# The FFN's second projection as seven half-block products, its steps placed between the next chunk's up-projection items

## Chip, cores and metric

The kernel runs on one core of one Trainium2 chip, in one launch. The metric is the device time of one execution in microseconds; lower is better. Before the change it is 1301.34 us, the median of three runs (1300.74 to 1302.6).

## The reference

The model is a decoder trunk with two layers, on 512 tokens of width 1024, all in fp32. Each layer has a token mixer (gated linear attention in the first, gated DeltaNet in the second) and then a feed-forward network, the FFN. This change touches the FFN and the residual ahead of it:

```python
def conv_ffn(x, w_in, conv_w, w_out):
    h = causal_dwconv(x @ w_in, conv_w)          # width 3, per channel
    gate, up = jnp.split(h, 2, axis=-1)
    return (jax.nn.gelu(gate, approximate=False) * up) @ w_out

h = layer_norm(ALPHA * h + y, ln_g[i, 0], ln_b[i, 0])                  # y: the mixer's output
h = layer_norm(ALPHA * h + conv_ffn(h, ...), ln_g[i, 1], ln_b[i, 1])
```

`w_in` is 1024 x 5632 and `w_out` 2816 x 1024. The hidden width 2816 is 22 blocks of 128.

## The kernel before

An fp32 product is made of three matmuls. Each operand is split into a high part, cast to fp32r on ACT (ScalarE), and a low part, the difference, taken on DVE (VectorE); PE (TensorE) adds high x high, high x low and low x high in one PSUM bank. So every weight costs one cast (L243, or L233 for pieces of 512 columns) and one subtraction (L244, L234), and so does every activation that is multiplied (`split_out`, L416 to L418).

The FFN (`ffn`, L646) works in two chunks of 12 and 10 blocks. For a block f there are two *items*, gate and up: 24 matmuls of 512 columns each (`fm_mms`, L286; the tiles are called `fm`), which leave one block of 128 channels by 512 tokens in one PSUM bank. `ffn_conv` (L637) applies the three taps of the convolution, one on ACT (L641) and two on DVE (L643). The gate goes through gelu on ACT (L653). The up item is multiplied by it on DVE (L658) and split into `gh` and `gl`.

When a chunk's items are done, `out_proj` (L370) multiplies its blocks by the rows of `w_out` that belong to them, for each half of the 1024 output columns and each of four blocks of 128 tokens (`tm_half`, L342; tiles `tm`). It adds the result to the residual `h` from PSUM (L379 the first time, L381 later). In the last chunk the last half ends token block by token block (`tail`, with `TAIL` = 4 weight pairs held in small slots, L229). Behind each token block come its statistics (L386) and the layer norm: `ln` (L542) transposes the result for the next stage, `ln_out` (L588) writes the output.

The weights follow one list, `plan`, in the order of use. `weight()` takes the next entry, and `prefetch` (L262) issues the load on SP's queue and the split for as many entries ahead as `look` says (2, or 8 near the end of an FFN), as long as fewer than `WB` = 4 weight buffers are held. Small work, such as a layer norm's, is a generator with due times that `pump` (L126) advances between matmuls by a planner's clock. After the first stage `pin` is off (L813). From there the order of an engine's instructions is that of the program only as far as the framework that compiles it keeps to it.

`ln` also prepares the residual for the FFN behind a mixer: scale and shift by the layer norm's parameters, two operations on POOL (GpSimd) for each half of a token block (L583, L584).

SBUF tiles of 128 x 512 fp32 come from one pool of 53 slots, and PSUM has eight banks.

## Time and profile before

| | |
|---|---|
| median of three runs | 1301.34 us |
| profiled execution, span on the core | 1300.2 us |
| PE busy, matmuls | 1279.0 us, 6666 |
| DVE, ACT, POOL busy | 790.2, 546.8, 111.0 us |
| first FFN on PE | from 241.1 to about 598 us |
| second FFN on PE | from 934.6 to about 1290 us |
| HBM read | 119.63 MB |

The profile is of one execution. Its page gives each engine's busy time, the chain of work that ended last (followed back from the last instruction), the costliest groups of instructions by line, engine and tile, and the DMA issues. The trace behind it can be asked for the chain in order of time, for the waits, for busy times by stretch and for single instructions. A row of a group reads: line, engine, operation, output<-input, shape and count | busy us in all, mean ns of one | idle time of the engine just before them, and what ended it. In a list of single instructions, the brackets at the end hold that idle time.

### The profile page before, as it was taken

What the parts mean: (1) busy time and instruction counts of PE and PEld (TensorE: products, weight loads), DVE (VectorE), ACT (ScalarE), POOL (GpSimd) and SP (SyncE); (2) the same over time, 40 slices, a digit from 0 to 9 for tenths busy, and PEclk for the clock granted to TensorE, in tenths of its full rate; (3) what the DMA queues carried; (4) which work ended last, traced back from release to release, by engine and by line L of the source; (5) the groups of instructions that cost most, each with busy time, mean ns of one, the idle gap of its engine ahead of it and who ended that gap; (6) DMA issues with size and microseconds to landing.
All of it is one profiled execution on the core that took longest, in us unless ns stands there. A gap on an engine that the chain in (4) does not pass through costs nothing.

```text
span 1300.2 us, 17238 instructions
## 1 busy us (share of the span) xinstructions
PE 1279.0 (98%) x6666; PEld 1078.1 (83%) x6666; DVE 790.2 (61%) x1442; ACT 546.8 (42%) x1030; POOL 111.0 (9%) x150
## 2 busy tenths in 40 slices
PE   8999999999999999999999999999999999999996
PEld 6878888988888888889788889988888888888885
DVE  3673366676643466655799835669677653366656
ACT  3554443634421344425865535543554431244420
POOL 4000000070000000001111310100034000000000
PEclk9999999999999999999999968999999999999999
DMA  6421224143333333251543420333143333333331
GB/s 181 117 81 49 77 86 130 33 130 114 98 97 97 97 97 98 87 143 66 135 117 106 127 49 17 115 98 113 49 137 107 97 98 98 97 97 97 97 98 65
DMA packets 167089, 126.52 MB, mean 97 GB/s; under 512 B 16088, under 2 KB 139546, under 8 KB 167008
## 3 DMA queue, kind: packets, MB, share of 16 engines
q1 hardware_dynamic: 161728, 115.10, 30.0%
q0 software_dynamic: 3888, 8.50, 2.1%
q10 hardware_dynamic: 1392, 1.84, 0.4%
q8 instruction: 52, 0.85, 0.3%
q14 instruction: 29, 0.24, 0.1%
HBM read 119.63 MB, written 5.78 MB: 96 GB/s over the span
## 4 chain that ended last, share of the span: by engine, by line
PE 86%; issue 6%; DVE 5%; DMA 1%; ACT 1%; POOL 1%; DVEq 0%; POOLq 0%; ACTq 0%
PE fm L155 45%; PE tm L155 32%; PE o L155 1%; PE V L155 1%; PE R L155 1%; PE xT L166 1%; PE vn L155 1%; DVE ln_st L386 1%; PE pg L155 1%; PE yT L166 1%; PE qkT L166 1%; PE pq L155 0%; DMA gla_nw<-in_gla_norm_w_dram 0%; DVE wl L244 0%; DVE conv L940 0%
## 5 line engine op out<-in xcount | busy, mean ns | idle before, releaser
L244 DVE TENSOR_TENSOR wl<-raw,wh 128x1024 fp32r<-128x1024 f32 (+1 forms) x190 | 238.3, 1255 | 321.1 <-ACT wh L243 319.3
L155 PE MATMUL fm<-xh,wh 128*128 128x512 f32 (+1 forms) x1104 | 408.3, 370 | 0.4 <-ACT wh L243 0.4
L155 PE MATMUL fm<-xl,wh 128*128 128x512 f32 (+1 forms) x1104 | 404.8, 367 | 0.0
L155 PE MATMUL fm<-xh,wl 128*128 128x512 f32 (+1 forms) x1096 | 401.2, 367 | 2.5 <-DVE wl L244 2.5
L243 ACT CAST wh<-raw 128x1024 fp32r<-128x1024 f32 (+1 forms) x190 | 198.8, 1047 | 269.9 <-PE tm L155 159.4
L155 PEld LDWEIGHTS fm<-xh,wl 128*128 128x128 f32 x1096 | 207.4, 190 | 36.5 <-DVE wl L244 3.1
L155 PEld LDWEIGHTS fm<-xh,wh 128*128 128x128 f32 x1104 | 209.1, 189 | 34.2 <-ACT wh L243 1.2
L155 PEld LDWEIGHTS fm<-xl,wh 128*128 128x128 f32 x1104 | 209.3, 190 | 32.7
L643 DVE SCALAR_TENSOR_TENSOR conv<-fm,ffn_cw,conv 128x511 f32<-128x511 f32 (+1 forms) x176 | 130.7, 745 | 3.0
L155 PE MATMUL tm<-wl,gh 128*128 128x512 f32 x288 | 112.0, 389 | 0.0
L155 PE MATMUL tm<-wh,gh 128*128 128x512 f32 x288 | 112.0, 389 | 0.0
L155 PE MATMUL tm<-wh,gl 128*128 128x512 f32 x288 | 112.0, 389 | 0.0
L155 PE MATMUL tm<-wh,xh 128*128 128x512 f32 x192 | 79.5, 414 | 1.0 <-ACT qk L756 1.0
L417 ACT CAST gh<-conv 128x512 fp32r<-128x512 f32 x44 | 27.3, 621 | 124.7 <-DVE conv L658 124.6
L155 PE MATMUL tm<-wh,xl 128*128 128x512 f32 x192 | 75.4, 393 | 0.0
L155 PE MATMUL tm<-wl,xh 128*128 128x512 f32 x192 | 75.1, 391 | 0.0
L653 ACT ACTIVATE conv<-conv 128x512 f32<-128x512 f32 x44 | 27.8, 633 | 95.0 <-DVE conv L643 95.0
L155 PEld LDWEIGHTS tm<-wh,gh 128*128 128x128 f32 x288 | 54.1, 188 | 11.2
L155 PEld LDWEIGHTS tm<-wh,gl 128*128 128x128 f32 x288 | 54.1, 188 | 11.2
L155 PEld LDWEIGHTS tm<-wl,gh 128*128 128x128 f32 x288 | 54.1, 188 | 11.2
L641 ACT ACTIVATE conv<-fm,ffn_cw 128x512 f32<-128x512 f32 x88 | 59.9, 681 | 0.2
L940 DVE SCALAR_TENSOR_TENSOR conv<-fm,gdn_cw,conv 128x509 f32<-128x509 f32 (+2 forms) x72 | 53.2, 742 | 4.6 <-ACT conv L938 4.1
(274 smaller groups left out, 1555.4 us busy)
## 6 DMA issues: line engine op xcount, KB each, us to landing
raw<-in_ffn_w_in_dram SPq DMA_DIRECT2D x88, 512.0 KB, 3.7
raw<-in_ffn_w_out_dram SPq DMA_DIRECT2D x44, 512.0 KB, 3.7
raw<-in_gdn_w_in_dram SPq DMA_DIRECT2D x32, 512.0 KB, 4.0
raw<-in_gla_w_in_dram SPq DMA_DIRECT2D x23, 512.0 KB, 3.5
raw<-in_gla_w_out_dram SPq DMA_DIRECT2D x8, 512.0 KB, 3.5
raw<-in_gdn_w_out_dram SPq DMA_DIRECT2D x8, 512.0 KB, 3.8
hd<-h POOLq DMA_DIRECT2D x8, 256.0 KB, 2.5
dt<-drow POOLq DMA_DIRECT2D x8, 256.0 KB, 5.6
```

The lines of the kernel that those rows point to most:

```text
L155: t = self.nc.tensor.matmul(out, a, b, start=start, stop=stop)
L166: t = self.nc.tensor.transpose(out, a, self.ident[:n, :n])
L243: nc.scalar.copy(wh[:, cols], raw[:, cols])
L244: nc.vector.tensor_sub(wl[:, cols], raw[:, cols], wh[:, cols])
L386: nc.vector.bn_stats(self.st[tb][:, hf, :], h)
L417: cast = self.nc.scalar.copy(dst_h, src)
L641: nc.scalar.activation(a, ps, AF.Identity, scale=tap(2))
L643: nc.vector.scalar_tensor_tensor(a[:, d:], ps[:, :S - d], tap(2 - d), a[:, d:], ALU.mult, ALU.add)
L653: nc.scalar.activation(a, a, AF.Gelu)
L940: self.conv = nc.vector.scalar_tensor_tensor(a[:, d:], ps[:, :S - d], tap(3 - d), a[:, d:], ALU.mult, ALU.add)
```

## The change

The second projection of blocks 0 to 17 is done in pairs of blocks, in chunks of three pairs. A pair is a 2 x 2 block product: the activations have two halves of 256 tokens by two blocks (x11, x12, x21, x22), the weights two blocks by two halves of 512 columns. In place of eight products of such half-blocks there are seven, of sums and differences. `combine` makes the activations' side on DVE: r = x21 - x22 (s1), r - x11 (s2), x11 - x21 (s3) and x12 + s2 (s4). It splits those together with x11, x12 and x22. The weights' sums are made by DMA: a load of one quarter on SP's queue and accumulating DMAs of other quarters on POOL's (`sums_plan`; four loads and four adds a pair).

The seven products run in four phases over the three pairs of a chunk (`sums_proj`): x11 and s1 into banks A and B, s2 and s4 into A and B, s3 and x12 into A and C, and x22 into A. A bank is folded into `h` on DVE after the phase in which a partial sum is complete (`fold`, 14 operations a chunk), and A and B are accumulated further after that. The eleven steps of a chunk (nine with two products, then x22 for two pairs and for one) stand between the up-projection items of the next chunk, in the order that `woven` gives. The last two pairs are multiplied as before (`last_proj`), both column halves of a token block one after the other.

There are four more edits. The weights' sums are fetched three plan entries ahead of their split (`fetch`, `AHEAD`), and `look` is 3. For some up-projection weights the low part is made by ACT (a negated copy) and an accumulating DMA instead of DVE (`BYDMA`: one item in chunk 0, four in each of chunks 1 and 2, one in the plain part). The residual's scale moves from POOL to DVE and its shift to an accumulating DMA. And the matmul helper lets a bank's accumulation group stay open.

```diff
-CHUNKS = ((0, 12), (12, 22))
+CHUNKS = ((0, 3), (3, 6), (6, 9))
+PLAIN = (9, 11)
+HALF = 2 * P
+AHEAD = 3
+BYDMA = 1
...
+    def sums_plan(self, w, rows):
+        nc = self.nc
+        n = len(rows)
+        a, b, c = ([None] * n for _ in range(3))
+        made = {}
+        def quad(i, r, col):
+            at = (rows[i] + r) * P
+            return w[at:at + P, blk(col, S)]
+        def load(t, i, r, col):
+            t[i] = self.slot("wq")
+            nc.sync.dma_start(t[i], quad(i, r, col))
+        def add(t, i, r, col):
+            nc.gpsimd.dma_start(t[i], quad(i, r, col), accum_op=ALU.add)
+        def duo(phase, of, *steps):
+            def begin():
+                for step, *args in steps:
+                    step(*args)
+            name = phase, of[-1][1]
+            behind = [made[phase - 1, i] for _, i in of] if phase else []
+            for _, i in of:
+                made[phase, i] = name, id(made)
+            return "duo", of, behind, (name, id(made)), begin
+        for i in range(n):
+            yield duo(0, [(a, i), (b, i)], (load, a, i, 0, 0), (load, b, i, 0, 1), (add, b, i, 0, 0))
+        for i in range(n):
+            yield duo(1, [(b, i), (c, i)], (load, c, i, 1, 1), (add, b, i, 1, 1))
+        for i in range(n):
+            yield duo(2, [(c, i), (a, i)], (add, c, i, 0, 1), (load, a, i, 1, 0))
+        for k in range(0, n, 2):
+            both = range(k, min(k + 2, n))
+            yield duo(3, [(b, i) for i in both], *((add, b, i, 1, 0) for i in both))
+    def fetch(self):
+        while self.fetched < min(len(self.plan), self.taken + self.look + AHEAD):
+            item = self.plan[self.fetched]
+            if item[0] == "duo":
+                if any(x not in self.cast for x in item[2]):
+                    break
+                item[4]()
+            self.fetched += 1
...
+        for j, t in enumerate(raws):
+            wh, wl = hi[:, blk(j, S)], lo[:, blk(j, S)]
+            nc.scalar.copy(wh, t)
+            nc.vector.tensor_sub(wl, t, wh)
+            self.vec(0.7)
+            out.append((wh, wl))
...
+        if item[0] == "duo":
+            self.cast.add(item[3])
+            return self.halves([t[i] for t, i in item[1]])
...
+        if item[0] == "fm" and item[3]:
+            nc.scalar.copy(wh, raw)
+            nc.scalar.mul(wl, raw, -1.0)
+            nc.gpsimd.dma_start(wl.bitcast(F32), raw, accum_op=ALU.add)
+            return [(wh[:, blk(j, S)], wl[:, blk(j, S)]) for j in range(2)]
...
+        for kind in order or "i" * (len(items) - start):
+            if kind == "s":
+                next(steps)
+                continue
+            if kind == "l":
+                self.look = TAIL + WB
+                continue
...
+    def sums_proj(self, xs, first):
+        nc = self.nc
+        n = len(xs)
+        fresh = set()
+        banks = {s: [self.psum("tm") for _ in range(2)] for s in "ABC"}
+        add, sub = ALU.add, ALU.subtract
+        def prod(bank, i, which, w, end):
+            for j in range(2):
+                ps, (xh, xl) = banks[bank][j], xs[i][which]
+                begin = (bank, j) not in fresh
+                fresh.add((bank, j))
+                xh, xl = xh[:, blk(j)], xl[:, blk(j)]
+                self.mm(ps, xh, w[0], begin, False, True)
+                self.mm(ps, xh, w[1], False, False, True)
+                self.mm(ps, xl, w[0], False, end, True)
+            self.pump()
+        def fold(bank, low, hf, op):
+            for j in range(2):
+                tb = 2 * low + j
+                h = self.h[tb][hf]
+                if first and (tb, hf) not in fresh:
+                    fresh.add((tb, hf))
+                    self.wait(("h", tb, hf))
+                    nc.vector.scalar_tensor_tensor(h, h, ALPHA, banks[bank][j], ALU.mult, op)
+                else:
+                    nc.vector.tensor_tensor(h, h, banks[bank][j], op)
+                self.vec(0.7, self.clk + 0.4)
+        for phase in ((("A", "x11", (0, 0, add)), ("B", "s1", (1, 1, add))),
+                      (("A", "s2", (0, 1, sub)), ("B", "s4", (0, 1, add))),
+                      (("A", "s3", (1, 1, sub)), ("C", "x12", (0, 0, add)))):
+            for i in range(n):
+                w = self.weight()
+                for (bank, which, to), wk in zip(phase, w):
+                    prod(bank, i, which, wk, i == n - 1)
+                    if i == n - 1:
+                        fold(bank, *to)
+                self.spend()
+                for _, which, _ in phase:
+                    xs[i][which] = None
+                yield
+        for k in range(0, n, 2):
+            for i, wk in zip(range(k, min(k + 2, n)), self.weight()):
+                prod("A", i, "x22", wk, i == n - 1)
+            if i == n - 1:
+                fold("A", 1, 0, add)
+            self.spend()
+            yield
...
-        gb = self.ln_gb()
         for hf in range(2):
-            nc.gpsimd.tensor_mul(h[hf], h[hf], gb[hf])
-            nc.gpsimd.tensor_add(h[hf], h[hf], gb[2 + hf])
-            self.set(("h", tb, hf))
-            yield 5.0
+            if self.gb is None:
+                self.gb = {}
+            if hf not in self.gb:
+                self.gb[hf] = self.slot("gb")
+                nc.sync.dma_start(self.gb[hf], self.gb_rows[0][blk(hf, S)].partition_broadcast(P))
+                yield 6.0
+            nc.vector.tensor_mul(h[hf], h[hf], self.gb[hf])
+            self.vec(0.7)
+            nc.gpsimd.dma_start(h[hf], self.gb_rows[1][blk(hf, S)].partition_broadcast(P), accum_op=ALU.add)
+            if tb == NTB - 1:
+                del self.gb[hf]
+            self.set(("h", tb, hf), 8.0)
+            yield 6.0
...
+    def woven(n, m):
+        return "".join(k for _, k in sorted([(i / n, "i") for i in range(n)] + [((i + 0.95) / m, "s") for i in range(m)]))
...
+        outs, order = (), None
+        for p0, p1 in CHUNKS + (PLAIN,):
+            items = iter([col + f * P for f in range(2 * p0, 2 * p1) for col in (0, DFF)])
+            for k, kind in enumerate(order or "i" * (4 * (p1 - p0))):
+                if kind == "i":
+                    self.plan_fm(w_in, next(items), k > 5 and k % 4 == BYDMA)
+                else:
+                    self.plan.append(next(outs))
+            outs = self.sums_plan(w_out, range(2 * p0, 2 * p1, 2))
+            order = self.next_order(p0)
+        for hf in range(2):
+            for f in range(2 * p0, 2 * p1, 2):
+                self.plan_tm(w_out, f * P, 2, hf * S, True)
+    def next_order(self, p0):
+        c = CHUNKS + (PLAIN,)
+        at = [p for p, _ in c].index(p0)
+        return self.woven(4 * (c[at + 1][1] - c[at + 1][0]), self.steps(c[at][1] - c[at][0])) if at + 1 < len(c) else None
...
+        steps, order = (), None
+        self.look = 3
+        for p0, p1 in CHUNKS + (PLAIN,):
+            xs, act, items = [], {}, []
+            plain = p1 == PLAIN[1]
+            for f in range(2 * p0, 2 * p1):
+                def gate(ps, f=f, act=act):
                     a = self.ffn_conv(ps, cw, f)
                     nc.scalar.activation(a, a, AF.Gelu)
                     act[f] = a
 
-                def up(ps, f=f):
+                def up(ps, f=f, act=act, xs=xs, plain=plain):
                     u = self.ffn_conv(ps, cw, NF + f)
                     nc.vector.tensor_mul(u, u, act.pop(f))
-                    t = self.slot("gh", F32R), self.slot("gl", F32R)
-                    self.split_out(*t, u)
-                    gs.append(t)
+                    if plain:
+                        t = self.slot("gh", F32R), self.slot("gl", F32R)
+                        self.split_out(*t, u)
+                        xs.append(t)
+                    elif f % 2 == 0:
+                        act["even"] = u
+                    else:
+                        xs.append(self.combine(act.pop("even"), u))
 
                 items += [gate, up]
-            self.fm_items(items)
-            last = ci == len(CHUNKS) - 1
-            if last:
-                self.drain()
-                self.ln_begin(li, g, b)
-                if out:
-                    self.ln_gb()
-            a = lambda c, tb: (gs[c][0][:, blk(tb)], gs[c][1][:, blk(tb)])
-            self.out_proj(a, f1 - f0, ci == 0, final if last else None)
+            self.fm_items(items, steps, order[:-4] + "l" + order[-4:] if plain else order)
+            steps = self.sums_proj(xs, p0 == 0)
+            order = self.next_order(p0)
+        self.drain()
+        self.ln_begin(li, g, b)
+        if out:
+            self.ln_gb()
+        self.last_proj(xs, final)
+    def last_proj(self, xs, final):
+        nc = self.nc
+        n = len(xs)
+        self.look = TAIL + WB
+        ws = [[x for _ in range(n // 2) for x in self.weight()] for _ in range(2)]
+        self.st = [None] * NTB
+        for tb in range(NTB):
+            st = self.st[tb] = self.small([P, 2, 6], "ln_st")
+            for hf in range(2):
+                ps = self.psum("tm")
+                h = self.h[tb][hf]
+                for c in range(n):
+                    self.tm_terms(ps, *(t[:, blk(tb)] for t in xs[c]), *ws[hf][c], c == 0, c == n - 1)
+                    self.pump()
+                nc.vector.tensor_add(h, h, ps)
+                nc.vector.bn_stats(st[:, hf, :], h)
+                self.vec(1.4, self.clk + 0.4)
+            self.spawn(final(tb))
+            self.pump()
+        self.look = LOOKAHEAD
+    def combine(self, e, o):
+        nc = self.nc
+        t0, t1 = slice(0, HALF), slice(HALF, S)
+        def halves(src, names):
+            hi, lo = self.slot("gh", F32R), self.slot("gl", F32R)
+            self.split_out(hi, lo, src)
+            return {k: (hi[:, t], lo[:, t]) for k, t in zip(names, (t0, t1))}
+        r = self.slot("gr")
+        nc.vector.tensor_sub(r[:, t0], e[:, t1], o[:, t1])
+        nc.vector.tensor_sub(r[:, t1], r[:, t0], e[:, t0])
+        x11 = self.slot("gx", F32R)
+        self.split_out(x11[:, t0], x11[:, t1], e[:, t0])
+        x = {"x11": (x11[:, t0], x11[:, t1])}
+        x |= halves(r, ("s1", "s2"))
+        d = self.slot("gd")
+        nc.vector.tensor_sub(d[:, t0], e[:, t0], e[:, t1])
+        nc.vector.tensor_add(d[:, t1], o[:, t0], r[:, t1])
+        x |= halves(d, ("s3", "s4"))
+        x |= halves(o, ("x12", "x22"))
+        return x
```

45 lines of the change are left out of this document (27 added, 18 removed).

## Prediction

> **What bounds the kernel now.** I read the page from the top: busy times first, then the chain that ended last.
>
> ```profile
> span 1300.2 us, 17238 instructions
> PE 1279.0 (98%) x6666; PEld 1078.1 (83%) x6666; DVE 790.2 (61%) x1442; ACT 546.8 (42%) x1030; POOL 111.0 (9%) x150
> PE 86%; issue 6%; DVE 5%; DMA 1%; ACT 1%; POOL 1%; DVEq 0%; POOLq 0%; ACTq 0%
> ```
>
> PE is busy nearly all the time and carries 86% of the chain, but a busy share alone does not show how dense the matmuls are. The chain in order of time does, for the first FFN (and the last stretch of the second):
>
> ```profile
> 241.12 126.81 PE fm L155 x630
> 367.94 65.28 PE tm L155 x288
> 433.22 108.80 PE fm L155 x480
> 542.02 43.52 PE tm L155 x192
> ...
> 1235.50 38.09 PE tm L155 x168
> ```
>
> Each piece begins where the one above ends (241.12 + 126.81 = 367.93, and so on): from 241 to 585 us no gap shows. Both forms have one rate: 65.28 / 288 = 0.2267 us a matmul (tm) and 108.80 / 480 = 0.2267 us (fm). Every matmul taken away here is 0.2267 us off the end, as long as nothing else becomes late. The windows say how much room the other engines have (columns: stretch, its length, busy time and count of PE, PEld, DVE, ACT, POOL, clock, DMA share, GB/s), and the list of who waited for whom says that PE hardly waits, never inside an FFN:
>
> ```profile
> 367.93:433.22 65.29, 65.29 (x290) 54.07 (x289) 21.94 (x23) 13.68 (x14) 0.00 (x0) 1.00 0.32 97
> 433.22:542.02 108.80, 108.80 (x481) 90.09 (x481) 64.42 (x77) 44.25 (x59) 0.00 (x0) 1.00 0.33 97
> ...
> PE fm L155 <- DVE wl L244: 2.5, 3, 1.3
> ```
>
> The clock is granted in full (1.00) in both. DVE is at 59% beside the up-projection and 34% beside the second projection: that is the room which the change spends.
>
> **The change part by part.** *Removed matmuls.* A pair of 128-row blocks of the second projection is now 2 blocks x 2 halves x 4 token blocks x 3 = 48 matmuls, as 8 products of 6. Seven products are 42. Nine pairs in each of two FFNs save 6 x 9 x 2 = 108 matmuls of the same shape, 108 x 0.2267 = **24.5 us**. The last two pairs stay at 48 each. [...] The trace's 226.7 ns is used.
>
> *Vector work that is added.* The rows:
>
> ```profile
> L244 DVE TENSOR_TENSOR wl<-raw,wh 128x1024 fp32r<-128x1024 f32 x188 | 237.0, 1261 | 319.9 <-ACT wh L243 318.0 <-DMA T<-dinvt 1.7
> L643 DVE SCALAR_TENSOR_TENSOR conv<-fm,ffn_cw,conv 128x510 f32<-128x510 f32 x88 | 65.7, 748 | 3.0
> L658 DVE TENSOR_TENSOR conv<-conv,conv 128x512 f32<-128x512 f32 x44 | 33.5, 762 | 1.6
> L418 DVE TENSOR_TENSOR gl<-conv,gh 128x512 fp32r<-128x512 f32 x44 | 31.7, 721 | 29.0 <-ACT gh L417 29.0
> L234 DVE TENSOR_TENSOR wsl<-raw,wsh 128x512 fp32r<-128x512 f32 x32 | 20.7, 684 | 6.5 <-ACT wsh L233 6.5
> L379 DVE SCALAR_TENSOR_TENSOR h<-h,tm 128x512 f32<-128x512 f32 x32 | 21.4, 683 | 13.9 <-PE tm L155 13.9
> L615 DVE TENSOR_TENSOR h<-h,gb x8: 676/678/681, 884.1 to 908.1; 128x512 f32<-128x512 f32 x8
> L878 DVE SCALAR_TENSOR_TENSOR sg<-o,gla_rr,sg 128x256 f32<-128x256 f32 x16 | 6.9, 479 | 0.1
> L243 ACT CAST wh<-raw 128x1024 fp32r<-128x1024 f32 x188 | 197.6, 1051 | 268.4 <-PE tm L155 159.4 <-PE fm L155 85.1 <-DMA raw<-in_ffn_w_in_dram 14.9
> L417 ACT CAST gh<-conv 128x512 fp32r<-128x512 f32 x44 | 27.3, 621 | 124.7 <-DVE conv L658 124.6
> ```
>
> A middle chunk (12 up-projection items, 11 steps, 3 pairs) is 12 x 24 + 3 x 42 = 414 matmuls, 93.8 us of PE. DVE in it: 8 wl x 1.261 = 10.1 (four are left to DMA); 24 taps x 0.748 = 18.0; 6 products x 0.762 = 4.6; three `combine`, each five half-width operations at the nearest row, 0.479, and three full splits at 0.721, = 3 x 4.56 = 13.7; 21 half weights x 0.684 = 14.4; 14 folds x 0.683 = 9.6. Together 70.4 us, 75% of 93.8. ACT: 16 x 1.051 (four of them the negated copies), then 30 casts, 18 activations and three half-width casts at about L417's 0.621: 48 us, half of the stretch. So on average both stay under PE. The tightest is chunk 0, whose PE time is only 65.3 us: I count 11 wl (13.9), taps 18.0, products 4.6, `combine` 13.7, the first six half weights 4.1, and eight residual products of L615's kind, 0.678 each (5.4): 59.7 us, 91%. There all eight PSUM banks are free for the items, so a late convolution does not stop PE. These edits cost nothing on the path; if that cover were gone, each us of DVE beyond PE's time would be a us.
>
> *Weights by accumulating DMA.* Seven operands come from four quarters by four loads on SP's queue and four accumulating adds on POOL's. No accumulating DMA is in the trace; the nearest rows (KB, then us to landing) are
>
> ```profile
> raw<-in_ffn_w_out_dram SPq DMA_DIRECT2D x44, 512.0 KB, 3.7
> hd<-h POOLq DMA_DIRECT2D x8, 256.0 KB, 2.5
> dt<-drow POOLq DMA_DIRECT2D x8, 256.0 KB, 5.6
> ```
>
> A chain of load and add is 3.7 + 2.5 to 3.7 + 5.6, so 6.2 to 9.3 us; I take the long one, since the add also reads what it writes. `fetch` runs three plan entries ahead of the cast, and an entry is 93.8 / 23 = 4.08 us of PE: 12.2 us of lead, and another 12.2 us from cast to use. So nothing on the path, at either end. Nothing can be gained here either: PE waits for no weight in an FFN now. The adds queue behind each other on POOL; its old work there, the residual's scale and shift, goes away (the scale to DVE, the shift to a DMA whose first reader is the third step of chunk 1). The adds for wl of four items a chunk are 512 KB from SBUF and have the same three entries.
>
> *Banks and folds.* Bank A is read after phases 1, 2, 3 and then accumulated further, bank B after the first and second. The next phase's first matmul must wait for the read. Walk the first such place of chunks 1 and 2, where an item with `combine` stands right before the folding step. Counting from the item's end, DVE owes ACT's 0.7 us, 1.5 taps, 0.76 product, 4.56 `combine`, 1.37 half weights, then the folds at 0.68: the first is over at 9.6 us, and at 10.8 if another wl slips in ahead. PE has the step (2.72) and an item (5.44) as cover, so it wants the bank at 8.2: a stall of 1.4 to 2.6 us. In the plain part two steps stand next to each other at that place: 0.7 + 1.5 + 1.37 + 0.68 = 4.3 us against 2.72: 1.6 us, 2.8 with a wl. In program order that is 2 x (2 x 2.6 + 2.8) = 16 us at the worst, 9 at the best. But program order does not hold in this part of the program:
>
> ```profile
> 257.12 0.69 DVE L658 TENSOR_TENSOR conv<-conv,conv 128x512 f32<-128x512 f32 x1
> 257.82 1.22 DVE L244 TENSOR_TENSOR wl<-raw,wh 128x1024 fp32r<-128x1024 f32 x1
> 258.96 0.68 DVE L418 TENSOR_TENSOR gl<-conv,gh 128x512 fp32r<-128x512 f32 x1
> ```
>
> The code issues L418 right behind L658; a weight split was put between while L418 waited for its cast. So folds can fill holes in `combine`, and PE can have the next item's matmuls put ahead of a blocked product. I take 0.5 us for each of six places, **+3 us**, and keep 0 and 16.
>
> *The end of each FFN.* Now both halves of a token block end together. Before, the first half's adds and statistics were done long before the tail; the DVE rows of the second FFN's tail:
>
> ```profile
> 1273.62 0.69 DVE L381 TENSOR_TENSOR h<-h,tm 128x512 f32<-128x512 f32 x1 [9.46 <-PE tm L155]
> ...
> 1279.44 0.68 DVE L381 TENSOR_TENSOR h<-h,tm 128x512 f32<-128x512 f32 x1
> 1280.15 0.69 DVE L386 BATCH_NORM_STATS2 ln_st<-h 128x6 f32<-128x512 f32 x1
> 1280.88 0.21 DVE L527 BATCH_NORM_AGGREGATE ln_mv<-ln_st 128x2 f32<-128x12 f32 x1
> ...
> 1295.53 1.42 DVE L594 SCALAR_TENSOR_TENSOR h<-h,ln_rs,gb 128x512 f32<-128x512 f32 x2
> ```
>
> From 1273.62 DVE does not idle: 1279.44 - 1273.62 = 5.82 us a token block, against 24 x 0.2267 = 5.44 on PE. DVE, not PE, ends the program. The change puts one more add and statistics (1280.88 - 1279.44 = 1.44 us) into three of these rounds; the first block's falls before 1273. **+4.3 us.** In the first FFN's tail DVE has holes:
>
> ```profile
> 585.58 0.69 DVE L381 TENSOR_TENSOR h<-h,tm 128x512 f32<-128x512 f32 x1 [1.40 <-PE tm L155]
> 591.96 0.69 DVE L381 TENSOR_TENSOR h<-h,tm 128x512 f32<-128x512 f32 x1 [1.01 <-PE tm L155]
> 598.46 0.69 DVE L569 TENSOR_TENSOR xl<-xf,xh 128x512 fp32r<-128x512 f32 x1 [1.40 <-ACT xh L568]
> 607.67 0.43 DVE L565 CAST xh<-xf 128x512 fp32r<-128x512 f32 x1 [3.34 <-ACT xf L561]
> ```
>
> Three extra rounds of 1.44 = 4.3 us meet holes of 1.40, 1.01 and 1.40 ahead of the last block: 0.5 us is left over, and I take **+0.9** (0 to 4.3) for the last block's layer norm, on which the next stage's second halves wait.
>
> *Sum:* -24.5 + 3.0 + 4.3 + 0.9 = -16.3 us. On the profiled span 1300.2 this gives 1283.9; the median of the runs is 1301.34, 1.1 us above that span, so **1285.0 us**.
>
> **The rivals.** (1) *The adds are late: slower.* If an accumulating DMA takes longer than 12.2 - 3.7 = 8.5 us, the cast of its result stands at the head of ACT's and DVE's queues and holds the convolutions behind it. DVE has 25% of an item and a step (8.16 us), 2.0 us, to spare. There are 66 steps; the 19.3 us that the rest leaves are used up at 0.29 us of PE time a step, so it decides at an add of about 10.8 us. At 11.2, twice the longest row above, it would be 0.7 us x 66 = 46 us, about 1328. For it: nothing here shows what an add costs. Against it: all rows are half of that. [...] Chance 0.10.
> (2) *Program order holds at the folds, or the 53 slots run out* (I count 8 residual, 9 raw quarters, some 26 combined halves and 8 in passing, 51 at the fullest), so that DVE waits for a PE step and PE for DVE: 9 to 16 us in place of 3, 1291 to 1298, at the worst 1301. Chance 0.21.
> (3) *All of it hides:* no stall at the banks, and the tails cost 0 to 5.2: 1277 to 1282. Chance 0.12.
> (4) The products don't become fewer on PE: about 1306, from the tails alone. Nothing speaks for it. Chance 0.02.
>
> **How the numbers follow.** The forecast, 1282 to 1290, has 0.55. A measurement of this kernel can tell 0.2%, 2.6 us, from no change. Under 1298.7 lie the forecast, rival 3 and most of rival 2 (0.16): 0.83. Within 0.2%: the worst of rival 2 and a mild rival 1, 0.07. Slower: 0.10. The range 1278 to 1298 holds the forecast, most of rival 3 and three quarters of rival 2, 0.81.
>
> **What would show it.** PE should have 6558 matmuls, the same 0.2267 us each, with `tm` and `fm` groups interleaved and gap-free through the middle chunks; idle time "PE tm <- DVE h" would be the fold stall, of 3 us in all. DVE's last four rounds should be 7.25 us apart. Accumulating adds on POOL's queue should land in under 8.5 us. I am wrong if ACT or DVE idle long for DMA into `wq`, if a middle chunk is over 96 us of wall time, or if the tail after PE's last matmul does not grow by about 4 us.

## The result, and the profile after

The changed kernel takes 1284.05 us (median of four runs, 1278.42 to 1285.42); the kernel before, run beside it, 1301.6 us. The ratio is 0.9854, with a 95% interval of 0.9832 to 0.9877: faster, by 17.5 us between the medians. The forecast was 1285.0 us, a saving of 16.3. Three runs of the kernels tried below took far longer at a low granted clock (2141.5 us at 0.56, 1555.9 at 0.75, 1393.8 at 0.84), and the ratios leave them out.

The profiled execution took 1284.87 us. Its page begins, with the shares of its chain of waits below:

```profile
span 1283.2 us, 17783 instructions
PE 1258.0 (98%) x6558; PEld 1060.1 (83%) x6558; DVE 872.2 (68%) x1704; ACT 611.3 (48%) x1176; POOL 152.2 (12%) x226
...
PE 82%; DVE 7%; DMA 2%; ACT 1%; issue 1%; SPq 0%; DVEq 0%; ACTq 0%; POOLq 0%
```

PE has 108 matmuls fewer and stays at 98%: most of what was taken off its busy time came off the span (17.0 of 21.0 us), while DVE took on 82.0 us and ACT 64.5 us without showing much more in the chain. The chain in order of time shows the new weave of items and steps, here at the start and, behind the dots, at the end of the second FFN's woven part (start, length, what):

```profile
1000.52 2.72 PE tm L161 x12
1003.24 5.44 PE fm L161 x24
...
1240.49 5.44 PE fm L161 x24
1245.93 9.53 PE tm L161 x42
```

A step is 12 matmuls in 2.72 us, an item 24 in 5.44 us: 0.2267 us each, the rate of before, and one begins where the other ends. The windows of the two middle chunks of the first FFN (stretch, length, busy time and count of PE, PEld, DVE, ACT, POOL, clock, DMA share, GB/s):

```profile
314.36:408.20 93.84, 93.84 (x415) 77.76 (x415) 64.28 (x101) 45.39 (x69) 14.18 (x17) 1.00 0.68 163
408.20:502.00 93.80, 93.80 (x415) 77.72 (x415) 61.62 (x97) 44.88 (x67) 13.72 (x16) 1.00 0.66 151
```

A middle chunk lasts exactly its 414 matmuls (414 x 0.2267 = 93.8 us). PE waited for nothing in it; DVE was busy 69% of the first. Inside the chunks the change is worth its full count. What PE still waits for, from the list of waits over the whole run (who <- for whom: us in total, times, longest):

```profile
PE xT L172 <- DVE h L698: 2.8, 2, 2.7
...
PE tm L161 <- ACT gh L563: 0.3, 1, 0.3
PE tm L161 <- DVE h L521: 0.3, 1, 0.3
```

So the folds (L521) stop PE for 0.3 us in all, and the largest new wait, 2.7 us, is for the layer norm at the end of the first FFN.

To see where the 17.0 us lie, I cut both traces at the same places: the first up-projection matmul of each FFN, the mixer's first one between them, and the last matmul of all (start times before: 234.64, 598.94, 928.07, 1289.51; after: 235.44, 591.43, 921.56, 1271.38).

| stage, us | before | after | difference | 54 matmuls fewer | left |
|---|---|---|---|---|---|
| up to the first FFN | 234.64 | 235.44 | +0.8 | | +0.8 |
| first FFN | 364.30 | 355.99 | -8.3 | -12.2 | +3.9 |
| mixer between | 329.13 | 330.13 | +1.0 | | +1.0 |
| second FFN, to its last matmul | 361.44 | 349.82 | -11.6 | -12.2 | +0.6 |
| from the last matmul's start to the end | 10.7 | 11.8 | +1.1 | | +1.1 |

The sum was right, but not by its own terms: the first FFN lost more than forecast, the folds and the program's end less.

### The profile page after: what moved, and what is told of

Read it like the earlier page. It is cut to its first block, busy times and chain, and to the rows that moved or that the text cites. A ratio compares the mean times of both kernels' runs of the same rounds, so it can differ in the third digit from the quotient of the medians.

```text
span 1283.2 us, 17783 instructions
## 1 busy us (share of the span) xinstructions
PE 1258.0 (98%) x6558; PEld 1060.1 (83%) x6558; DVE 872.2 (68%) x1704; ACT 611.3 (48%) x1176; POOL 152.2 (12%) x226
## 4 chain that ended last, share of the span: by engine, by line
PE 82%; DVE 7%; DMA 2%; ACT 1%; issue 1%; SPq 0%; DVEq 0%; ACTq 0%; POOLq 0%
PE fm L161 43%; PE tm L161 29%; PE o L161 2%; PE R L161 1%; PE V L161 1%; DMA wq<-in_ffn_w_out_dram 1%; PE xT L172 1%; DVE conv L1166 1%; DVE wl L322 1%; PE pg L161 1%; PE vn L161 1%; PE yT L172 1%; PE qkT L172 1%; PE s L161 0%; PE qs L161 0%
## 5 line engine op out<-in xcount | busy, mean ns | idle before, releaser
L322 DVE TENSOR_TENSOR wl<-raw,wh 128x1024 fp32r<-128x1024 f32 (+1 forms) x134 | 162.6, 1215 | 142.1 <-ACT wh L321 139.0
L321 ACT CAST wh<-raw 128x1024 fp32r<-128x1024 f32 (+1 forms) x134 | 139.7, 1043 | 200.8 <-PE fm L161 107.9
L266 ACT CAST wh<-wq 128x512 fp32r<-128x512 f32 x126 | 74.7, 619 | 110.9 <-DMA wq<-in_ffn_w_out_dram 37.5
L267 DVE TENSOR_TENSOR wl<-wq,wh 128x512 fp32r<-128x512 f32 x126 | 84.9, 687 | 61.8 <-ACT wh L266 61.3
L224 POOL DMA_DIRECT2D wq<-in_ffn_w_out_dram x72 | 63.0, 901 | 263.2 <-DVE wl L267 150.2
L161 PE MATMUL tm<-wh,gh 128*128 128x512 f32 x216 | 84.4, 391 | 0.3 <-DVE h L521 0.3
L161 PE MATMUL tm<-wl,gh 128*128 128x512 f32 x216 | 84.2, 390 | 0.0
L161 PE MATMUL tm<-wh,gl 128*128 128x512 f32 x216 | 84.2, 390 | 0.0
L317 POOL DMA_DIRECT2D wl<-raw x20 | 17.5, 875 | 442.0 <-ACT wl L316 425.4
L521 DVE TENSOR_TENSOR h<-h,tm 128x512 f32<-128x512 f32 x68 | 44.9, 683 | 34.8 <-PE tm L161 34.8
```

Source lines behind the costliest of these rows:

```text
L161: t = self.nc.tensor.matmul(out, a, b, start=start, stop=stop, skip_group_check=open_group)
L224: nc.gpsimd.dma_start(t[i], quad(i, r, col), accum_op=ALU.add)
L266: nc.scalar.copy(wh, t)
L267: nc.vector.tensor_sub(wl, t, wh)
L317: nc.gpsimd.dma_start(wl.bitcast(F32), raw, accum_op=ALU.add)
L321: nc.scalar.copy(wh[:, cols], raw[:, cols])
```

## The experiments

Runs of one and the same kernel differ here by up to 1% (the kernel before, from 1291.8 to 1304.1 us in one series), and their spans go with the granted clock (1290.0 us at 0.995, 1302.4 at 0.984). A good part of the difference between profiles lies in a stage that no edit touches: in the mixer between the FFNs the clock was 0.95 in the changed kernel's profile (330.1 us), 0.97 in two other profiles (324.1 us) and 0.99 in one (318.6 us), for the same work. So besides the ratio, each run below is read by the two FFN stages and the end of its own profile. In the two stages the clock was 1.00 but for stretches of 0.50 near waits of PE; the column "half clock" has the sum of these stretches, and up to half of it is part of the difference. All are the changed kernel but for the edit; us, with the sum of the three differences from the changed kernel in the last column.

| run | first FFN | mixer | second FFN | end | half clock | ratio to before, 95% interval | FFNs and end |
| --- | --- | --- | --- | --- | --- | --- | --- |
| changed kernel | 355.99 | 330.13 | 349.82 | 11.8 | 0 | 0.9854 (0.9832 to 0.9877) |  |
| put_back | 368.91 | 328.23 | 361.93 | 11.8 | 3.4 | 1.0054 (1.0026 to 1.0082) | +25.0 |
| no_weave | 378.01 | 325.62 | 377.20 | 11.8 | 41.0 | 1.0221 (1.0175 to 1.0266) | +49.5 |
| no_weave_kept | 363.20 | 330.18 | 357.71 | 11.8 | 0 | 1.0000 (0.9967 to 1.0034) | +15.2 |
| pinned | 357.39 | 324.13 | 351.00 | 11.8 | 0 | 0.9897 (0.9848 to 0.9946) | +2.6 |
| ahead0 | 360.27 | 324.06 | 353.15 | 11.8 | 3.4 | 0.9924 (0.9894 to 0.9954) | +7.6 |
| no_bydma | 357.29 | 330.17 | 349.99 | 11.8 | 3.4 | 0.9888 (0.9853 to 0.9923) | +1.5 |
| resid_pool | 364.18 | 318.57 | 355.99 | 11.5 | 3.4 | 0.9958 (0.9925 to 0.9991) | +14.1 |
| reserve | 359.48 | 329.85 | 350.20 | 11.8 | 6.8 | 0.9889 (0.9852 to 0.9926) | +3.9 |
| cap | 360.74 | 329.00 | 349.39 | 11.8 | 3.4 | 0.9891 (0.9840 to 0.9941) | +4.3 |
| ln_later | 352.19 | 330.63 | 349.23 | 11.8 | 0 | 0.9851 (0.9815 to 0.9888) | -4.4 |
| tail_dma | 368.95 | 329.77 | 358.26 | 11.8 | 23.9 | 0.9992 (0.9969 to 1.0015) | +21.5 |
| five_sixths | 360.79 | 329.44 | 347.98 | 18.5 | 8.0 | 0.9922 (0.9899 to 0.9945) | +9.7 |

My theory after the result: TensorE's count is the gain and comes through whole in the chunks; the folds cost nothing because the compile step moves work past them; the rest went in the tails. Rivals: the gain is the placing and not the count; the accumulating transfers cost time; VectorE's new work costs time.

### Putting the 108 matmuls back (put_back)

```diff
                 self.mm(ps, xh, w[1], False, False, True)
+                if which in ("x11", "s2", "s3"):
+                    self.mm(ps, xl, w[1], False, False, True)
                 self.mm(ps, xl, w[0], False, end, True)
```

> Each pair of three of the seven sums (x11, s2, s3) gets a fourth matmul for each block, low part times low part, so that the 108 matmuls that the seven products saved are issued again, in the same banks, with the same weights, loads, adds and vector work. Theory (the products' count is what was gained, TensorE being the bound all through the chunks, and some 7 us of it are lost again in the two tails): 108 x 0.2267 = 24.5 us more than the changed kernel, 1308.5 us (1306 to 1311), that is 7 us above the kernel before. Rival (the gain came from placing the steps between the items, and the count matters little): well under 1301, about 1284 to 1292.

The two FFN stages grew by 12.9 and 12.1 us, 25.0 against 24.5 expected (the half clock behind a wait in the first FFN's tail is up to 1.7 of them), and the kernel is slower than before by a ratio of 1.0054. The count is the whole gain; all else in the change costs 0.26% to 0.82% of the time, 3.4 to 10.7 us.

### All steps in a row (no_weave, no_weave_kept)

```diff
-        return "".join(k for _, k in sorted(...))
+        return "s" * m + "i" * n
```

> The seven products stay; all steps of a chunk come in a row ahead of the next chunk's items, and no longer between them. Theory (the items between the steps are what hides the folds, the combined operands and the chain of load, add and split of a quarter): a step of 2.72 us then follows a step, a phase of three steps lasts 8.2 us, and load and add alone take 5.9 + 5.2 = 11.1 us in the median; at the chunk's end the combined halves of its last pair are some 8 us of VectorE work that only two steps cover. 2 to 8 us at each of six chunk ends, and up to 3 us at each of four phases: 1296 to 1332 us, with ACT waiting for the quarters' transfers and TensorE for ACT. Rival (the look-ahead and the compile step's own reordering are enough): 1284 within 3 us.

> As the run with all steps in a row ahead of the items, but the record of which sums have been split is kept apart for each chunk; in that run an add could be issued ahead of the split that still needed the old sum, so that some of its products had other weights, of the same number and size. Theory (placing the steps between the items is what hides the chain of load, add and split): the adds now wait for the split of the phase before, three steps or 8.2 us ahead of their use at most, against 11.1 us of load and add, so the time rises above that run's 1327 us, to 1330 to 1370. Rival (the 40 us are the combined operands of the chunk's last pair and the fold, and the adds are no part of it): within 4 us of 1327.

In the second run the record `made`, whose identity names a chunk's sums, is kept for all chunks, so that an add no longer goes ahead of the split that needs the old sum. It cost 15.2 us beside the changed kernel, nearly all that the whole change brings: its time is that of the kernel before. Of the first run's 49.5 us, 34.3 thus come from the adds put ahead of splits, not from the placing: there ACT waited 71.7 us for `wq`, 10.2 us at the longest, against 23.4 us in the second, and there are 41.0 us at half clock, up to 20.5 of the 49.5 us. Both expectations for the second run were wrong, mine by its sign. With the adds in order, PE's waits are these:

```profile
PE tm L162 <- DVE h L523: 3.6, 4, 0.9
...
PE tm L162 <- ACT gx L565: 2.4, 2, 1.6
...
PE tm L162 <- DVE h L521: 1.8, 2, 0.9
```

(This kernel's lines are two further down than the changed kernel's.) They are for the folds (`h`, 5.4 us) and for the last pair's combined operands (`gx`), in the rows of steps. Placing the steps between the items hides the vector work, not the transfers. All of the 15.2 us lies in the six rows: from the last up-projection matmul ahead of a row to the first behind it are 30.7 to 33.4 us, where 127 distances of 0.2267 us are 28.8. The waits shown make 7.8 us of it; what the rest is stays open.

### TensorE's order kept as written (pinned)

```diff
+            self.pin = True
             self.fm_items(items, steps, ...)
...
+        self.pin = False
         self.drain()
```

> TensorE's instructions of the FFN's chunks keep their order as written; the compile step may still move the other engines' work. Theory (the fold's wait of 0.3 us in all, where 3 us were predicted, is because the compile step put matmuls of the next item ahead of a step that follows a step): the waits for the fold come back where two steps stand in a row, in the plain part, 1 to 2 us at three or four places of each FFN: 6 to 12 us, 1290 to 1296, as waits of tm for DVE h. Rival (the fold is hidden by the banks alone, or by VectorE doing the fold first): 1284 within 2 us.

It cost 2.6 us in the two stages, between the two expectations and nearer to the rival. The trace of the changed kernel has the reordering, where two steps stand next to each other in the first FFN's plain part:

```profile
515.25 0.39 PE L161 MATMUL tm<-wh,gl 128*128 128x512 f32 x1
515.47 0.39 PE L161 MATMUL fm<-xh,wh 128*128 128x512 f32 x1
...
516.61 0.39 PE L161 MATMUL fm<-xh,wl 128*128 128x512 f32 x1
516.87 0.51 PE L161 MATMUL tm<-wh,gh 128*128 128x512 f32 x1
```

Six `fm` matmuls of the next item stand ahead of the step that needs the folded bank. In the pinned kernel PE stands at that step, and the list of waits has it twice, once for each FFN:

```profile
518.11 0.50 PE L161 MATMUL tm<-wh,gh 128*128 128x512 f32 x1 [1.01 <-DVE h L521]
```

```profile
PE tm L161 <- DVE h L521: 2.0, 2, 1.0
```

So the reordering is real and saves about 2 us. The other four places that the prediction counted, the first folding steps of the middle chunks, do not stall even in the order as written.

### The transfers' lead, and the low parts by DMA (ahead0, no_bydma)

```diff
-AHEAD = 3
+AHEAD = 0
```

> The quarters' loads and adds are issued no earlier than the split of the same step (three plan entries less lead). Theory (the accumulating transfers cost nothing because they have a lead of some 24 us, against 11.1 us that load and add take in the median and up to 20 with the queue's wait): with three entries, about 12.2 us, ACT stands in its queue at the split until the add has landed, and the convolutions' first ops behind it come late: 20 to 100 us more, 1304 to 1384. Rival (lead is no matter, another 12 us lie between the split and the matmul): 1284 within 3 us.

It cost 7.6 us (up to 1.7 of them the half clock behind the tail's wait), more than the rival allows and far less than I expected. Without the early start ACT does stand longer for the quarters, and only little of it reaches PE:

```profile
ACT wh L266 <- DMA wq<-in_ffn_w_out_dram: 79.0, 29, 5.7
...
PE tm L161 <- DVE wl L267: 3.2, 5, 1.3
```

In the changed kernel ACT stood 37.5 us for `wq` (16 times, 4.3 at the longest) and PE never for `wl` of a quarter. The lead matters, but the three entries between split and use take up most of a late add.

```diff
-BYDMA = 1
+BYDMA = 4
```

> VectorE makes the low parts of all the up-projection's weights, also of the five items of each FFN whose low part the changed kernel makes by ACT and an accumulating transfer. Theory (VectorE has 30% of its time left in the chunks, so those 10 x 1.22 us for each FFN are hidden; that edit is worth nothing): the stages of both FFNs within 1 us of 356.0 and 349.8. Rival (VectorE's work in the chunks decides at the folds and the combined operands): 2 to 8 us more, with TensorE waiting for wl or for h at the folds.

The stages grew by 1.3 and 0.2 us. The first is just past the bound of 1 us, but PE's waits in the chunks are the changed kernel's, and so is the 2.7 us wait for the layer norm in the tail. Behind that wait the clock was at half for 3.4 us (0.83 in the mean of the next 10 us, 1.00 in the changed kernel), and 1.7 us of matmuls lost by that are more than the whole difference. So no cost of undoing that edit is left to see: it is worth nothing that these profiles show.

### The residual on POOL again (resid_pool)

```diff
-            nc.vector.tensor_mul(h[hf], h[hf], self.gb[hf])
-            nc.gpsimd.dma_start(h[hf], self.gb_rows[1][...], accum_op=ALU.add)
+            nc.gpsimd.tensor_mul(h[hf], h[hf], gb[hf])
+            nc.gpsimd.tensor_add(h[hf], h[hf], gb[2 + hf])
...
```

> The scale and shift of the residual go back to POOL's two multiplies and adds for each half, as in the kernel before; all else is as changed. Theory (that edit is worth little by itself: VectorE has some 30% of its time left and the multiply was hidden, 0): within 1.5 us of the changed kernel, with POOL busy some 20 us more for each FFN. [...]

The FFN stages grew by 8.2 and 6.2 us, where the theory had 1.5 at the most. In each FFN PE's longest wait for weights is 60 us behind its start, and the others follow in the second chunk. Of PE's new waits 2.5 us are for an add ("PE fm <- DMA wl<-raw", twice), and the rest are for VectorE. The timeline of DVE and then of POOL (start, duration):

```profile
273.69 1.53 DVE L807 SCALAR_TENSOR_TENSOR conv<-fm,ffn_cw,conv 128x511 f32<-128x511 f32 x2 [1.57 <-ACT conv L805]
275.26 17.89 DVE L826 TENSOR_TENSOR conv<-conv,conv 128x512 f32<-128x512 f32 x1
293.08 2.28 DVE L322 TENSOR_TENSOR wl<-raw,wh 128x1024 fp32r<-128x1024 f32 x1
```

```profile
274.83 1.64 POOL L730 TENSOR_TENSOR h<-h,gb 128x512 f32<-128x512 f32 x1
...
292.67 1.60 POOL L730 TENSOR_TENSOR h<-h,gb 128x512 f32<-128x512 f32 x1
```

One VectorE multiply, 0.69 us in the median, took 17.89 us: from just after the start of POOL's second operation until just after the start of its last. The second FFN has the same (17.75 us). All that stands behind it on DVE comes late, and PE waits for weights: "PE fm <- DVE wl" is 10.0 us in eight waits, against 2.4 in three. This small edit, which the prediction priced as 5.4 us of VectorE's time and no more, is worth 14.1 us in the changed kernel (up to 1.7 of them are the half clock behind the tail's wait), beside 17.0 us of span for the whole change.

### The first FFN's tail (reserve, cap, ln_later, tail_dma)

The changed kernel's PE stands in the first tail at these rows (the transposes of the first block's layer norm):

```profile
574.78 0.39 PE L161 MATMUL tm<-wsh,gl 128*128 128x512 f32 x1
577.86 1.09 PE L172 MATMUL xT<-ident,h 128*128 128x128 f32 x8 [2.69 <-DVE h L698]
578.70 0.48 PE L161 MATMUL tm<-wsh,gh 128*128 128x512 f32 x1
```

Matmul starts are 3.08 us apart there, and 0.73 us at 565.8, where 0.23 would do: together 3.35 of the 3.9 us that this stage lost. Why does PE stand there, and did not before? VectorE's rows, first of the kernel before and then of the changed one, from the first add of that block to the scaling that PE waits for:

```profile
580.13 0.69 DVE L381 TENSOR_TENSOR h<-h,tm 128x512 f32<-128x512 f32 x1 [3.13 <-PE tm L155]
...
583.63 0.54 DVE L552 TENSOR_SCALAR h<-h,ln_mv,ln_rs 128x512 f32<-128x512 f32 x1
```

```profile
569.45 1.22 DVE L322 TENSOR_TENSOR wl<-raw,wh 128x1024 fp32r<-128x1024 f32 x1
570.59 1.28 DVE L869 TENSOR_TENSOR h<-h,tm 128x512 f32<-128x512 f32 x2
...
575.21 0.69 DVE L869 TENSOR_TENSOR h<-h,tm 128x512 f32<-128x512 f32 x1
...
577.26 0.54 DVE L698 TENSOR_SCALAR h<-h,ln_mv,ln_rs 128x512 f32<-128x512 f32 x1
```

The block's last product starts at 579.71 before and at 569.34 after. Counted from there the scaling ended after 4.5 us before, and ends after 8.5 us now: a weight split stands ahead of the adds, and the next block's adds (575.21 is one) and statistics stand between the layer norm's operations. The transposes have not moved: in both traces they stand 48 products into the tail, 24 behind their block's last. Two edits were to bring VectorE's work forward, one by leaving a weight buffer free, one by holding back the mixer's weights.

```diff
-            if self.held == WB and not self.in_slots(item) or ...
+            if self.held >= (WB - 1 if self.look == TAIL + WB else WB) and not self.in_slots(item) or ...
```

> In the last items and the plain part one of the four weight buffers is left free when weights are split ahead. Theory A (the first FFN's tail lost some 3 us because ACT stood 4 us in its queue for a weight buffer, a convolution's first op behind it, so that VectorE's work came late): ACT's idle time there goes, TensorE's wait for the first layer norm falls from 2.7 us to under 1, and the stage from the first FFN's first matmul to the mixer's falls from 356.0 to 353 or 354 us; some 1281.5 in all. Theory B (VectorE is late because it makes four splits for the mixer's weights, 4.9 us, ahead of the last folds and adds): 355.5 to 356.5, 1284.

```diff
                 self.plan_tm(w_out, f * P, 2, hf * S, True)
+        self.caps.append(len(self.plan))
...
         self.look = 3
+        self.cap = self.caps.pop(0)
...
         for tb in range(NTB):
+            if tb == 1:
+                self.cap = 1 << 30
+                self.prefetch()
```

> The mixer's weights aren't loaded or split until the first block of the first FFN's last products is done. Theory B: the four splits of 1.22 us are out of VectorE's way ahead of the first block's layer norm; TensorE's wait of 2.7 us for it goes to under 0.5 and that of 0.7 us for the plain part's operand too: the stage from the first FFN's first matmul to the mixer's falls from 356.0 to 353 us, 1281 in all. Theory A: VectorE's lateness stays, the stage stays at 355 to 356. A third way (the mixer's first weights then come too late, 20 us after): 357 or more, with TensorE waiting for wl at the mixer's start.

(The first edits are in `ffn_plan` and `ffn`, the last in `last_proj`; `fetch` and `prefetch` do not go past `cap`.) Both were misses: the stage became longer, by 3.5 and 4.8 us, and PE waited 4.3 us for that layer norm in the one, and 6.0 us in three waits for layer norms in the other. But neither trace has what its edit was to bring about. In reserve ACT stands as long as in the changed kernel, and in cap the four splits of the mixer's weights are made as early as before, the last of them at 569.7, ahead of the first layer norm (second row: count, shortest, median and longest ns, first and last start):

```profile
548.20 0.62 ACT L266 CAST wh<-wq 128x512 fp32r<-128x512 f32 x1 [4.07 <-issue]
```

```profile
L323 DVE TENSOR_TENSOR wl<-raw,wh x4: 1214/1221/1225, 561.9 to 569.7; 128x1024 fp32r<-128x1024 f32 x4
```

So these two runs do not tell what the weight buffer or the four splits cost; how much of VectorE's delay is due to the splits stays open. Much of the growth is the clock: after its wait TensorE ran on below full clock. The windows of reserve around the wait:

```profile
571.00:577.00 6.00, 1.72 (x8) 1.22 (x7) 5.90 (x28) 0.81 (x1) 0.42 (x1) 0.78 0.29 82
577.00:587.00 10.00, 10.00 (x40) 8.31 (x39) 5.32 (x10) 4.22 (x10) 1.97 (x4) 0.79 0.29 107
```

Ten us at 0.79 are 2.1 us of matmuls not done. (In the changed kernel the clock after its wait of 2.7 us was 1.00.)

```diff
-        yield ready - self.clk + 0.2
+        yield ready - self.clk + 0.2 + (self.late if tb == 0 else 0.0)
...
         self.st = [None] * NTB
+        self.late = 4.0
```

> In the first FFN's tail the transposes of the first block's layer norm are written 4 us later among TensorE's matmuls; nothing else is moved. Theory D (VectorE's layer norm chain for a block lasts longer than the 5.44 us of the next block's matmuls, and TensorE stands only because the transposes were put 15 matmuls after the block's end): the wait of 2.7 us goes, the stage from the first FFN's first matmul to the mixer's falls from 356.0 to 353 or 353.5 us. Theory C (VectorE, 36.0 of 39.7 us busy there, bounds the whole tail): the wait returns at the next transposes, the stage stays at 355 to 357.

The stage fell to 352.19 us. The wait of 2.7 us is gone from the list, with VectorE's operations in nearly the same order and the scaling as late (8.5 us behind the start of the block's last product); the first transposes stand 39 products behind it instead of 24 (not 15, as I had counted):

```profile
PE xT L173 <- DVE h L699: 0.2, 1, 0.2
```

364.30 less 54 matmuls is 352.06: the first FFN now keeps its whole saving, and the second (349.23 against 349.20) too. So VectorE was late, but what cost the time was the place of the transposes in TensorE's order: there was other work that it could do first. The span was 1279.1 us, the lowest of these profiles, with the mixer at its usual 330 us. The timed runs can't tell it from the changed kernel (0.9851 against 0.9854, the intervals overlap); its 4.4 us rest on one profile of each. The median of the runs in its ratio, 1278.4 us, is the lowest of all, on a chip where the kernel before took 1298.6.

```diff
+                if item[5] == "dma":
+                    nc.scalar.mul(wl, raw[:, blk(j, S)], -1.0)
+                    nc.gpsimd.dma_start(wl.bitcast(F32), raw[:, blk(j, S)], accum_op=ALU.add)
```

> The low parts of the plain part's weights, 16 splits of 0.68 us on VectorE for each FFN, are made by ACT (negated rounding) and an accumulating transfer, as the low parts of five items of each FFN are. Theory C (VectorE's work bounds the first tail): 11 us less of it, the stage from the first FFN's first matmul to the mixer's falls by 2.5 to 3.8 us from 356.0, the second FFN's stage and end by 0 to 1. Theory D: the wait for the first layer norm shrinks only by what comes off ahead of it, 1 to 2 us. Against both: 16 more adds on POOL's queue that land after 5 us or more make the plain part's weights late, 357 or more, with TensorE waiting for wsl.

The last line of that expectation came true: 368.95 us, 13 more, and 8.4 more in the second FFN. The waits:

```profile
PE tm L161 <- ACT gh L567: 6.9, 2, 5.1
PE tm L161 <- DMA wsl<-raw: 4.4, 3, 2.7
PE xT L172 <- DVE h L702: 4.1, 2, 4.0
```

Here an accumulating transfer is not free. PE waits for the transfers themselves (`wsl`) and for operand splits (`gh`) that come late because the weights ahead of them on ACT's queue do: ACT stood 4.0 us in the first FFN and 8.6 in the second for the last load of `w_out`, against 2.2 and 2.8 in the changed kernel. That these loads are late because the transfers still read the buffers they go to fits this, but is not tested. Up to 12 of the 21.5 us are the half clock behind the waits.

### One more pair by seven products (five_sixths)

```diff
-CHUNKS = ((0, 3), (3, 6), (6, 9))
-PLAIN = (9, 11)
+CHUNKS = ((0, 4), (4, 7), (7, 10))
+PLAIN = (10, 11)
```

> The run with the later transposes, with one more pair of each FFN by seven products: chunks of four, three and three pairs, and one pair plain. Rival (the products' count goes on paying): 12 matmuls fewer, 12 x 0.2267 = 2.7 us less than that run's span of 1279.1, 1276.4. Theory (two pairs are left plain because their items cover the last chunk's steps, and their products the layer norms): in the plain part there are four items for eleven steps, so three steps stand in a row, and a block's last products last 2.72 us against some 6 to 7 us of VectorE's work for a block's adds, statistics and layer norm. Folds and late quarters cost 1 to 3 us for each FFN, the first FFN's tail 3 to 8, the second's 2 to 6: 1284 to 1296 in all, with waits of xT for DVE and of tm for DVE h or ACT at the places named.

It took 1290.48 us, as expected. Beside ln_later, on which it is built, the second FFN fell by 1.25 us (six matmuls are 1.36), so the steps in rows of three cost nothing, against my theory. The tails cost more than I thought: +8.6 us in the first FFN (up to 4.0 of them the half clock), where PE waits for the layer norms of one block after the other, and +6.7 us at the end (18.5 against 11.8), with no more of PE's products to lie over VectorE's rounds.

```profile
PE xT L173 <- DVE h L699: 5.7, 4, 2.7
```

```profile
582.00:592.00 10.00, 4.45 (x23) 3.28 (x22) 10.00 (x46) 6.00 (x13) 2.20 (x4) 0.78 0.28 105
592.00:602.00 10.00, 9.88 (x61) 9.47 (x62) 6.41 (x15) 9.97 (x28) 2.14 (x4) 0.71 0.28 105
```

DVE is busy for all of the ten us in which PE is at 45%. Here VectorE does bound the tail, and behind the waits the clock (0.78 and 0.71) adds to it. Two plain pairs are the better choice.

## Why the prediction was right

- *Removed matmuls, -24.5.* Shown: 108 matmuls put back cost 25.0 us, and 23.3 at the least if the half clock took its most.
- *Vector work that is added, 0.* Right: DVE was busy 64.3 us in a middle chunk, where I had 70.4 (the half-width operations took 0.42 us, not 0.479, and other rows were shorter too), and PE never waited. What the step missed is what the residual's move to VectorE is worth, which I priced only as 5.4 us of DVE time in chunk 0: undone, it costs 14.1 us, so without that move 0 would have been far off.
- *Weights by accumulating DMA, 0.* Right in the sum. Issues and landings:

```profile
wq<-in_ffn_w_out_dram SPq DMA_DIRECT2D x72, 256.0 KB, 5.9
wq<-in_ffn_w_out_dram POOLq DMA_DIRECT2D x72, 256.0 KB, 5.2
wl<-raw POOLq DMA_DIRECT2D x20, 512.0 KB, 4.8
```

  An add of 256 KB landed after 5.2 us, inside my 2.5 to 5.6; the load took 5.9, where I had 3.7 from a row of twice the size. The chain, 11.1 us, is above my 9.3 and nearly the 12.2 us of lead. Rival 1 was nearer than I thought, but with the lead gone the loss was 7.6 us and not of the order of the 46 that I had for an add of 11.2 us: I had let every us by which an add is late hold the convolutions, and the split stands three entries ahead of its use. My sign for being wrong, ACT idle for `wq`, did appear (37.5 us) and meant nothing, since PE had no wait from it. POOL's adds took 0.90 us each to issue (72 of them, 63.0 us), beside a VectorE that was busy 69% of the first middle chunk.
- *Banks and folds, +3.0.* Mis-sized: 0.3 us of waits. The two places in the plain parts are saved by reordering (2.0 us of waits when it was forbidden); the four in the middle chunks do not stall in any order.
- *The end of each FFN, +4.3 and +0.9.* Both mis-sized, in opposite ways. At the program's end the cost was 1.1 us, and so my sign for being wrong, a tail that does not grow by about 4 us, did come true; it told of a mis-sized term, not of a wrong sum. From the first block's second add to DVE's end it was 23.33 us before (1273.62 to 1296.95) and 24.41 after (1255.49 to 1279.90):

```profile
1258.63 0.21 DVE L683 SCALAR_TENSOR_TENSOR ln_t<-ln_rs,ln_var 128x1 f32<-128x1 f32 x1
1258.77 0.68 DVE L869 TENSOR_TENSOR h<-h,tm 128x512 f32<-128x512 f32 x1
1259.36 0.15 DVE L684 SCALAR_TENSOR_TENSOR ln_rs<-ln_t,ln_rs 128x1 f32<-128x1 f32 x1
1259.48 0.69 DVE L870 BATCH_NORM_STATS2 ln_st<-h 128x6 f32<-128x512 f32 x1
1260.09 0.20 DVE L683 SCALAR_TENSOR_TENSOR ln_t<-ln_rs,ln_var 128x1 f32<-128x1 f32 x1
1260.33 0.16 DVE L684 SCALAR_TENSOR_TENSOR ln_rs<-ln_t,ln_rs 128x1 f32<-128x1 f32 x1
```

  The extra add and statistics (L869, L870) were put between the layer norm's tiny operations, each of which needs the one before. Without something between, the next starts 0.24 us after (1260.09 to 1260.33); with it, the tiny one costs 0.14 (1258.63 to 1258.77) and the wide one 0.59. The blocks' rounds also run into each other: their last operations lie 8.91, 5.21 and 3.39 us apart, where I had 7.25 each. That this interleaving is why the 4.3 us shrank is read from these rows, not tested. At the end of the first FFN it was 3.9 us where I had 0.9: I had looked for holes on DVE ahead of the last block, and the cost was a wait of PE for the first block's layer norm, which now ends 8.5 us behind its products instead of 4.5, with the transposes where they stood before. With them later the cost is gone.

The errors of the terms, -2.7 and -3.2 against +3.0, nearly cancelled, and the stages without an edit added 1.8 us that no term could hold. That the sum came within 1 us owes something to this, and that is luck; that the sign and the size were right owes to the first term, which carried it.

## What to carry to other kernels

Where the traces show an engine dense, price a removed instruction at its start-to-start distance, and look for the loss not inside the loop but at its ends, where the removed work was the cover of something else: with one more pair the tails ate more than the products saved. TensorE here stood for an operand that nothing needed yet, while products that it could have done stood behind the transposes: the place of one block's transposes was worth 3.8 us. Look in the trace whether an edit moved what it was to move before its time is read: two of these runs did not move it. Before an idle sign is used to test a theory, ask whether anyone waits behind it.

## What the runs showed of the hardware

- In resid_pool a VectorE multiply with two inputs in SBUF took 17.89 us while POOL worked through a row of multiplies and adds. In the kernel before, with the same POOL work, it was only slowed, to 1.47 us (0.69 alone) and 2.30 us (1.23 alone):

```profile
274.45 1.47 DVE L658 TENSOR_TENSOR conv<-conv,conv 128x512 f32<-128x512 f32 x1
...
277.56 2.30 DVE L244 TENSOR_TENSOR wl<-raw,wh 128x1024 fp32r<-128x1024 f32 x1
```

  What holds the multiply, and why for a whole row of POOL's operations here and not before, stays open.
- The same wait of TensorE in the first FFN's tail, 2.69 us, stands in six profiles. Over the 10 us behind it the granted clock was 0.83 to 0.86 in four (ahead0, no_bydma, resid_pool, cap) and 1.00 in two (the changed kernel, pinned); behind the 4.28 us of reserve it was 0.76. In no_bydma it was 0.51 from 578.0 to 581.4 us and 1.00 on both sides; its matmuls of 512 columns start 0.43 us apart from 579.37 to 581.08, and 0.23 from 581.49 on. Why the same wait was followed by it in four profiles and not in the other two, no run here shows.
- The mixer's clock, 0.95 to 0.99 with nothing changed, moved a run by up to 12 us, more than most of the experiments. What sets it, no run here shows.
